# Other orders for the matmuls of the block products and of two mixer stages

## The chip, the core and the metric

The kernel runs on one core of one Trainium2 chip. The metric is the device time of one execution in microseconds, the median of several runs. TensorE (PE) does the matmuls, VectorE (DVE), ScalarE (ACT) and GpSimd (POOL) the elementwise work, SyncE (SP) issues DMAs. All engines run their own instruction streams and meet at semaphores.

## The reference

One layer of a streaming encoder, in fp32, for a prompt of 512 frames and 64 frames of a running stream, 1024 features:

```python
def encoder_layer(x, hist_a, hist_b, ...):
    x = x + 0.5 * swiglu_ffn(rms_norm(x, ffn1_norm), ffn1_w_gate_up, ffn1_w_down)
    h = rms_norm(x, mix_norm)
    p = h @ w_in
    a_b, a_c, a_v, b_u, gate_a, gate_b = jnp.split(p, cuts, axis=-1)
    a_conv, new_a = causal_depthwise_conv(a_c * a_v, hist_a, conv_a_w)
    y_a = (a_b * a_conv) @ w_a_out
    glu = b_u[..., :D_B] * jax.nn.sigmoid(b_u[..., D_B:])
    b_conv, new_b = causal_depthwise_conv(glu, hist_b, conv_b_w)
    b_act = jax.nn.silu(layer_norm(b_conv + conv_b_bias, conv_b_ln_g, conv_b_ln_b))
    y_b = b_act @ w_b_out
    merged = jax.nn.sigmoid(gate_a) * y_a + jax.nn.sigmoid(gate_b) * y_b
    x = x + merged @ w_out
    x = x + 0.5 * swiglu_ffn(rms_norm(x, ffn2_norm), ffn2_w_gate_up, ffn2_w_down)
```

A final `rms_norm` follows. `D_FF` is 2816; `w_in` has seven blocks of 1024 columns. The histories of both convolutions are outputs too.

## The kernel before

Features lie on the 128 rows, the T = 576 frames on the columns, in two halves of H = 288 columns (`HALVES`). An input `X[j]` is one of KT = 8 tiles of 128 features. To keep fp32 accuracy with the fast fp32r matmul, each operand is split into a high and a low part, and a product is the sum of three: high weights times high input, high weights times low input, low weights times high input. In the code these are `parts` 0, 1 and 2, or `m` 0, 1 and 2.

An ordinary product (`product`, `mm`) makes 128 output features for both halves. It takes the 8 feature tiles of its input one after the other, and for each runs six matmuls, part n on half s, in the order `SIX`: (0,0), (1,0), (0,1), (1,1), (2,0), (2,1). The first half adds into one PSUM bank, the second into the next bank of the same tile. Each such product has 48 matmuls of 288 columns in the FFN's first tiles and in the mixer, and 30 or 36 in the down projections.

The mixer's stages are: `("p", 4, j)` and `("p", 3, j)` for branch B; `("p", 1, j)`, `("p", 2, j)` and `("p", 0, j)` for branch A, 24 products; `("p", 5, j)` with `("ya", j)`; `("p", 6, j)`, 8 products; `("yb", j)`; `("o", j)`. Between some of them a sum over features is made with four matmuls against a tile of ones (`Sum.total`).

The gate and up products of the FFNs work in pairs (`pair`): for output tile i, both parts together are made from seven block products over half the feature tiles (KU = 4), a scheme of the Strassen kind. Each block product has a weight unit of its own, streams one half of the columns into one bank, and has twelve matmuls: four tiles k times three parts m. `Forms.operands` says which half each of the seven streams: first, second, first, first, first, second, second, in the order in which they run. The FFN's 22 output tiles form four groups (`GROUPS`: 5, 5, 6 and 6); the first 3 tiles of the first FFN and the first tile of the second are ordinary products (`PLAIN`). After each group the down projection of that group runs.

Weights come through `Stream`: SyncE loads a raw unit of 256 KB, ScalarE casts the high part, and the low part is made either by VectorE or, for units marked "dma", by ScalarE negating the high part and GpSimd issuing a DMA that adds the raw weights to it. `ws.get(n)` prepares six units ahead of the one asked for. All instructions stay in program order on their engine (`Ordered`); `dve.time` and `pe.time` are a planner's counts that decide when work put off (`work`, `behind`) is placed. They depend on the number and width of the matmuls, not on their order.

Where the profile names L80, that is the helper through which all instructions are recorded; buffers are told apart by name: `mm` are PSUM tiles, `act` are inputs (and in the mixer also weights), `u` and `g` are weights.

Of the kernel before, what the change touches and what calls it, by code (L numbers as in the profile page):

```python
# [17 lines left out]
FT = DFF // P  # L18
SEQ = 512
DSEQ = 64  # L20
KU = KT // 2
# [23 lines left out]
HALVES = ((0, H), (H, T))  # L45
# [8 lines left out]


SIX = ((0, 0), (1, 0), (0, 1), (1, 1), (2, 0), (2, 1))

RAWS = 6

# [44 lines left out]
def tile_encoder_step(  # L104
# [284 lines left out]
    plan_ffn("f2", ffn2_gu, ffn2_dn)  # L389


    def mm(ps, w, kk, xs, first, last, spans=HALVES):


        (whi, wlo), (xh, xl) = w, xs
        parts = ((whi, xh), (whi, xl), (wlo, xh))
        for n, s in SIX:
            if s < len(spans):
                (a, b), (i, e) = parts[n], spans[s]
                pe.matmul(  # L400
                    ps[:, s, : e - i], a[:, kk, :], b[:, i:e],
                    start=first and n == 0, stop=last and n == 2,
                )

    def chunks(name):
# [25 lines left out]
    def product(name, xs, then=None, order=None, got=None):  # L431

        if name in early:
            return early.pop(name)[:, :, :H]
        ps = psum2()
        if order or got:
            got = got or chunks(name)
            for n, k in enumerate(order or range(len(xs))):
                mm(ps, *got[k], xs[k], n == 0, n == len(xs) - 1)
        else:  # L440
            k = 0
            for n in plan[name]:
                w = ws.get(n)
                for kk in range(ws.units[n][1]):
                    mm(ps, w, kk, xs[k], k == 0, k == len(xs) - 1)
                    k += 1
        take()
        if then is None:
            dve.time = max(dve.time, pe.time)
            return ps[:, :, :H]  # L450
        fill()
        behind.append((pe.time, lambda: then(ps[:, :, :H])))
# [205 lines left out]
    first = {name: psum2() for name in FIRST}  # L658
# [31 lines left out]
    def ffn(f, xg, sums, finish, forms, R=None, todo=()):  # L690
# [41 lines left out]
                for step, p in todo.pop(0):  # L732
                    step(p)

        def pair(i, hs, last):
            qu, uu, t, cu = (ttile() for _ in range(4))
            q1, u2, u3, u4 = half(qu, 0), half(qu, 1), half(uu, 0), half(uu, 1)
            q = []

            def q7():  # L740
                dve.tensor_tensor(u3, q[3], u2, op=ALU.add)
                dve.tensor_tensor(half(cu, 1), u3, q[2], op=ALU.subtract)

            def gate():
                dve.tensor_tensor(half(t, 1), q[5], u4, op=ALU.add)
                dve.tensor_tensor(t, t, R, op=ALU.mult)
                sca.activation(t, t, AF.Silu)

            steps = (
                lambda: sca.copy(q1, q[0]),  # L750
                lambda: dve.tensor_tensor(u2, q[1], q1, op=ALU.subtract),
                lambda: dve.tensor_tensor(u4, q[2], u2, op=ALU.subtract),
                q7,
                lambda: dve.tensor_tensor(half(t, 0), q[4], q1, op=ALU.add),
                gate,
            )
            for n, xs in enumerate(bs):
                w = ws.get(plan[f, "s", i][n])
                q.append(bank()[:, :H])
                for k in range(KU):  # L760
                    (whi, wlo), (xh, xl) = w, xs[k]
                    for m, (l, r) in enumerate(((whi, xh), (whi, xl), (wlo, xh))):
                        pe.matmul(
                            q[n], l[:, k, :], r, start=k == m == 0, stop=k == KU - 1 and m == 2
                        )
                if n > 0:
                    steps[n - 1]()
                if rest:
                    rest.pop(0)()

            hs.append(None)
            at = len(hs) - 1

            def up():
                if last:
                    dve.tensor_tensor(t, t, R, op=ALU.mult)
                dve.tensor_tensor(half(cu, 0), q[6], u3, op=ALU.add)

            def hidden():
                dve.tensor_tensor(cu, cu, t, op=ALU.mult)  # L780
                hs[at] = high(cu)

            def parts():
                hs[at] = hs[at], low(cu, hs[at])

            rest.extend((up, hidden, parts))

        for g, grp in enumerate(GROUPS):
            hs = []
            for i in grp:  # L790
                if i < PLAIN[f]:
                    plain(i, hs)
                    continue
                if i == PLAIN[f]:
                    bs = forms.operands(xg)
                pair(i, hs, grp[-1] == FT - 1)
            while rest:
                rest.pop(0)()
            spare.clear()
            if grp[-1] < FT - 1:  # L800
                for j, ps in enumerate(both([(f, "d", g, j) for j in range(2)], hs)):
                    update(j, ps, R)
                for j in range(2, KT):
                    update(j, product((f, "d", g, j), hs), R)
            else:
                finish(g, hs)
# [390 lines left out]
```

## Time and profile before

| | us |
|---|---|
| median of 3 runs | 1302.38 (1302.33 to 1303.26) |
| profiled execution | 1303.07 |
| its span | 1301.3 |
| TensorE busy | 1286.3 |
| VectorE busy | 892.0 |
| ScalarE busy | 778.5 |
| GpSimd busy | 400.5 |

The span runs from the first to the last instruction; the rest of an execution's time lies around it. The granted clock of TensorE was 0.998 of full speed. A row of the list of stretches gives start and end in us from the span's start, the length, TensorE's busy time and the number of matmuls that touch the stretch, the granted clock, the share of the DMA engines and GB/s. A row of time gives start, length, engine, line, operation, tiles and the number of instructions merged in it. A matmul's own length (some 294 ns) contains its passage through the pipeline, so speed is read from start to start or from a stretch's length over its matmuls.

### The profile page before, as it was taken

Reading aid. Unit: us, or ns where it says so; the run is one execution under the profiler, and the core shown is the slowest. Engines: PE = TensorE matmul, PEld = TensorE weight load, DVE = VectorE, ACT = ScalarE, POOL = GpSimd, SP = SyncE. Lnnn points to the kernel's source line nnn. Section 1 sums busy time; section 2 is a strip of 40 time slices with the busy share of each in tenths; the row PEclk is TensorE's granted clock in tenths of the full one; section 3 lists DMA queues with packets and bytes.
Section 4 is the critical chain, followed back from the end, with each engine's and each line's share of the span. In section 5 each row is a group of like instructions: output and inputs, shape, how many; then the busy total and the mean of one; then the engine's idle time right before and its main releaser. Section 6 shows DMA issues by size and latency. Waiting matters only on the chain.

```text
span 1301.3 us, 25714 instructions
## 1 busy us (share of the span) xinstructions
PE 1286.3 (99%) x9746; PEld 1282.5 (99%) x9746; DVE 892.0 (69%) x1460; ACT 778.5 (60%) x1374; POOL 400.5 (31%) x502
## 2 busy tenths in 40 slices
PE   9999999999999999999999999999999999999997
PEld 8999999999999999999999999999999999999996
DVE  6758758748945899888895260336967848847955
ACT  8755655645677655555554684457665655654664
POOL 4242332332242544322221322222142141241233
PEclk9999999999999999999999999999999999999999
DMA  9797787886798797877775978776687796796784
GB/s 245 141 189 160 148 185 157 165 192 147 152 195 182 167 216 173 175 166 170 172 168 125 199 158 178 154 166 142 138 169 165 162 192 149 163 206 136 161 178 107
DMA packets 290108, 218.40 MB, mean 168 GB/s; under 512 B 15680, under 2 KB 251200, under 8 KB 289984
## 3 DMA queue, kind: packets, MB, share of 16 engines
q0 software_dynamic: 60768, 100.30, 46.4%
q1 hardware_dynamic: 227488, 115.62, 31.4%
q8 instruction: 77, 1.26, 0.4%
q10 hardware_dynamic: 1728, 0.84, 0.2%
q14 instruction: 47, 0.39, 0.1%
HBM read 113.81 MB, written 2.62 MB: 89 GB/s over the span
## 4 chain that ended last, share of the span: by engine, by line
PE 90%; issue 4%; DMA 2%; ACT 1%; POOL 1%; DVE 1%; DVEq 0%; POOLq 0%; ACTq 0%; SPq 0%
PE mm L80 90%; DMA g<-raw 1%; DMA raw<-in_ffn_w_gate_up_dram 1%; POOL act L80 1%; DVE tmp L80 0%; ACT u L80 0%; DMA gains<-in_params_dram 0%; POOL g L80 0%; ACT tmp L80 0%; ACT g L80 0%; DVE acc L80 0%; ACT act L80 0%; DVE x L80 0%; DVE g L80 0%; POOL tmp L80 0%
## 5 line engine op out<-in xcount | busy, mean ns | idle before, releaser
L80 PE MATMUL mm<-act,u 128*128 128x288 f32 x4686 | 660.9, 294 | 0.7 <-DVE u L80 0.5
L80 PEld LDWEIGHTS mm<-act,u 128*128 128x128 f32 x4686 | 630.9, 188 | 1.2 <-DVE u L80 0.7
L80 PE MATMUL mm<-act,g 128*128 128x288 f32 x2766 | 398.6, 294 | 2.1 <-DMA g<-raw 2.0
L80 PEld LDWEIGHTS mm<-act,g 128*128 128x128 f32 x2766 | 376.5, 188 | 2.9 <-DMA g<-raw 2.8
L80 POOL DMA_DIRECT2D u<-raw x204 | 176.3, 864 | 550.4 <-ACT u L80 492.2
L80 PE MATMUL mm<-act,act 128*128 128x288 f32 (+2 forms) x2244 | 307.6, 293 | 1.4 <-DVE act L80 1.4
L80 PEld LDWEIGHTS mm<-act,act 128*128 128x128 f32 x2244 | 297.8, 188 | 2.4 <-DVE act L80 2.1
L80 POOL DMA_DIRECT2D g<-raw x124 | 108.6, 876 | 247.2 <-ACT g L80 188.2
L80 ACT CAST u<-raw 128x512 fp32r<-128x512 f32 (+2 forms) x204 | 117.1, 574 | 108.6 <-PE mm L80 76.5
L80 DVE SCALAR_TENSOR_TENSOR w<-g,prm,w 128x606 f32<-128x606 f32 x232 | 179.3, 844 | 1.4 <-ACT w L80 1.4
L80 DVE TENSOR_TENSOR tmp<-mm,tmp 128x288 f32<-128x288 f32 (+1 forms) x244 | 109.7, 458 | 72.9 <-PE mm L80 53.5
L80 ACT ACTIVATE u<-u 128x512 fp32r<-128x512 f32 (+2 forms) x204 | 121.1, 594 | 6.5
L80 POOL DMA_DIRECT2D act<-raw x90 | 78.9, 876 | 50.6 <-ACT act L80 49.5
L80 DVE SCALAR_TENSOR_TENSOR tmp<-mm,r 128x576 f32<-128x576 f32 x48 | 36.3, 757 | 78.0 <-PE mm L80 77.8
L80 ACT CAST g<-raw 128x512 fp32r<-128x512 f32 (+2 forms) x124 | 67.7, 546 | 35.3 <-DMA raw<-in_ffn_w_down_dram 14.7
L80 ACT CAST act<-tmp 128x576 fp32r<-128x576 f32 x84 | 56.2, 674 | 52.4 <-DVE tmp L80 51.6
L80 ACT CAST g<-w 128x512 fp32r<-128x512 f32 x80 | 49.6, 619 | 63.0 <-DVE w L80 56.6
L80 ACT CAST u<-w 128x512 fp32r<-128x512 f32 x80 | 49.5, 619 | 61.9 <-DVE w L80 55.7
L80 DVE TENSOR_TENSOR act<-tmp,act 128x576 fp32r<-128x576 f32 x80 | 59.3, 754 | 21.3 <-ACT act L80 19.8
L80 ACT ACTIVATE g<-g 128x512 fp32r<-128x512 f32 (+2 forms) x124 | 70.4, 568 | 3.9
L80 ACT CAST act<-raw 128x512 fp32r<-128x512 f32 (+2 forms) x99 | 57.6, 583 | 16.1 <-PE mm L80 11.0
L80 DVE TENSOR_TENSOR w<-raw,raw 128x512 f32<-128x512 f32 x80 | 54.8, 685 | 11.0 <-DMA raw<-in_ffn_w_gate_up_dram 11.0
(88 smaller groups left out, 814.1 us busy)
## 6 DMA issues: line engine op xcount, KB each, us to landing
raw<-in_ffn_w_gate_up_dram SPq DMA_DIRECT2D x173, 256.0 KB, 3.4
u<-raw POOLq DMA_DIRECT2D x145, 256.0 KB, 4.0
raw<-in_w_in_dram SPq DMA_DIRECT2D x112, 256.0 KB, 3.4
act<-raw POOLq DMA_DIRECT2D x80, 256.0 KB, 4.8
raw<-in_ffn_w_down_dram SPq DMA_DIRECT2D x96, 192.0 KB, 3.5
g<-raw POOLq DMA_DIRECT2D x65, 256.0 KB, 3.8
g<-raw POOLq DMA_DIRECT2D x43, 192.0 KB, 4.5
u<-raw POOLq DMA_DIRECT2D x43, 192.0 KB, 4.5
```

Source lines behind the costliest of these rows:

```text
L80: return self.tc.keep_in_program_order(fn(*args, **kwargs))
```

## The change

The order of matmuls becomes a parameter. `mm` takes `six`; the three branch-A stages `("p", 1)`, `("p", 2)`, `("p", 0)` get `BACK`, the stage `("p", 6)` gets `PAIRED`, all others keep `SIX`. `pair` takes `twelve`, one order for each group of each FFN. The first group of the first FFN gets `BY_TILE`, which is the order of before. The flags that open and close an accumulation follow the order.

```diff
+BACK = ((0, 0), (1, 0), (1, 1), (0, 1), (2, 1), (2, 0))
+PAIRED = ((0, 0), (1, 0), (0, 1), (1, 1), (2, 1), (2, 0))
+
+BY_TILE = tuple((k, m) for k in range(KU) for m in range(3))
+SAME_INPUT = tuple((k, m) for k in range(KU) for m in (0, 2, 1))
+TO_AND_FRO = tuple((k, m) for k in range(KU) for m in ((1, 0, 2), (2, 0, 1))[k % 2])
+LOW_LAST = tuple((k, m) for ms in ((0, 1), (2,)) for k in range(KU) for m in ms)
+BY_PART = tuple((k, m) for m in range(3) for k in range(KU))
+LOW_FIRST = tuple((k, m) for k in range(KU) for m in (2, 0, 1))
+TWELVE = {
+    "f1": (BY_TILE, SAME_INPUT, TO_AND_FRO, LOW_LAST),
+    "f2": (BY_PART, LOW_FIRST, SAME_INPUT, TO_AND_FRO),
+}
...
-    def mm(ps, w, kk, xs, first, last, spans=HALVES):
+    def mm(ps, w, kk, xs, first, last, spans=HALVES, six=SIX):
         (whi, wlo), (xh, xl) = w, xs
         parts = ((whi, xh), (whi, xl), (wlo, xh))
-        for n, s in SIX:
+        opens = {s: n for n, s in reversed(six)}
+        closes = {s: n for n, s in six}
+        for n, s in six:
             if s < len(spans):
                 (a, b), (i, e) = parts[n], spans[s]
                 pe.matmul(
                     ps[:, s, : e - i], a[:, kk, :], b[:, i:e],
-                    start=first and n == 0, stop=last and n == 2,
+                    start=first and n == opens[s], stop=last and n == closes[s],
                 )
...
-                    mm(ps, w, kk, xs[k], k == 0, k == len(xs) - 1)
+                    six = {("p", 1): BACK, ("p", 2): BACK, ("p", 0): BACK, ("p", 6): PAIRED}
+                    mm(ps, w, kk, xs[k], k == 0, k == len(xs) - 1, six=six.get(name[:2], SIX))
...
-                for k in range(KU):
-                    (whi, wlo), (xh, xl) = w, xs[k]
-                    for m, (l, r) in enumerate(((whi, xh), (whi, xl), (wlo, xh))):
-                        pe.matmul(
-                            q[n], l[:, k, :], r, start=k == m == 0, stop=k == KU - 1 and m == 2
-                        )
+                whi, wlo = w
+                for at, (k, m) in enumerate(twelve):
+                    xh, xl = xs[k]
+                    l, r = ((whi, xh), (whi, xl), (wlo, xh))[m]
+                    pe.matmul(q[n], l[:, k, :], r, start=at == 0, stop=at == len(twelve) - 1)
...
-                pair(i, hs, grp[-1] == FT - 1)
+                pair(i, hs, grp[-1] == FT - 1, TWELVE[f][g])
```

The instructions of VectorE, ScalarE, GpSimd and SyncE stand in the same order as before. Two places on TensorE show what moves. The first is the seventh block product of the second pair of the second FFN (group order `BY_PART`): the out tile, the streamed input, the weights; `g_11646` is the high and `g_11647` the low part of the weights, made by DMA. Before:

```order
L80 MATMUL mm_11760<-act_10932,g_11646 128x288
L80 MATMUL mm_11760<-act_11092,g_11646 128x288
L80 MATMUL mm_11760<-act_10932,g_11647 128x288
L80 MATMUL mm_11760<-act_11088,g_11646 128x288
L80 MATMUL mm_11760<-act_11254,g_11646 128x288
L80 MATMUL mm_11760<-act_11088,g_11647 128x288
```

And now, to the first with the low part:

```order
L94 MATMUL mm_11760<-act_10932,g_11646 128x288
L94 MATMUL mm_11760<-act_11088,g_11646 128x288
L94 MATMUL mm_11760<-act_11250,g_11646 128x288
L94 MATMUL mm_11760<-act_11339,g_11646 128x288
L94 MATMUL mm_11760<-act_11092,g_11646 128x288
L94 MATMUL mm_11760<-act_11254,g_11646 128x288
L94 MATMUL mm_11760<-act_11343,g_11646 128x288
L94 MATMUL mm_11760<-act_11347,g_11646 128x288
L94 MATMUL mm_11760<-act_10932,g_11647 128x288
```

The low part of the weights was read by the third matmul and is now read by the ninth.

The second place is the first product of branch A, `("p", 1, 0)`, order `BACK`, the first of its eight feature tiles; `u_6356` and `u_6357` are the high and low part of the weights, `act_5411` and `act_5419` those of the first input tile, and a row with x2 is the same pair of tiles on one half and then on the other. Before:

```order
L80 MATMUL mm_6576<-act_5411,u_6356 128x288
L80 MATMUL mm_6576<-act_5419,u_6356 128x288
L80 MATMUL mm_6576<-act_5411,u_6356 128x288
L80 MATMUL mm_6576<-act_5419,u_6356 128x288
L80 MATMUL mm_6576<-act_5411,u_6357 128x288 x2
```

And now:

```order
L94 MATMUL mm_6576<-act_5411,u_6356 128x288
L94 MATMUL mm_6576<-act_5419,u_6356 128x288 x2
L94 MATMUL mm_6576<-act_5411,u_6356 128x288
L94 MATMUL mm_6576<-act_5411,u_6357 128x288 x2
L94 MATMUL mm_6576<-act_5414,u_6356 128x288
```

The low part of the input is now streamed on both halves in a row, and the high part on the second half with both parts of the weights in a row. The halves, which the rows don't show, run first, first, second, second, first, second before, and first, first, second, second, second, first now. `PAIRED` has the same sequence of halves; its rows read like those of `SIX`, with the two matmuls of the x2 row exchanged.

2 lines of the change are left out of this document (1 added, 1 removed).

## The prediction

> **What bounds the kernel now.** I read the page first: the shares, then who waits for whom, then the speed of the bounding engine stage by stage.
>
> ```profile
> span 1301.3 us, 25714 instructions
> PE 1286.3 (99%) x9746; PEld 1282.5 (99%) x9746; DVE 892.0 (69%) x1460; ACT 778.5 (60%) x1374; POOL 400.5 (31%) x502
> ...
> PEclk9999999999999999999999999999999999999999
> ```
>
> TensorE is busy in 99% of the span; VectorE, next, in 69%. There are 9746 weight loads for 9746 matmuls: each matmul loads its weights, also where they are those of the matmul before. The list of waits of TensorE, whole span:
>
> ```profile
> PE mm L80 <- DMA g<-raw: 2.0, 2, 1.5
> PE mm L80 <- DVE act L80: 1.7, 3, 0.8
> PE mm L80 <- POOL eps L80: 1.0, 1, 1.0
> PE mm L80 <- DVE acc L80: 0.5, 1, 0.5
> PE mm L80 <- DVE u L80: 0.5, 1, 0.5
> ```
>
> All of it is 5.7 us. So an order of matmuls can act in two ways: on a wait, or on the spacing of matmuls that follow without one. For the spacing I took stretches that begin and end with a stage, whose matmuls the program counts (the counts in the rows have two or three more, which overlap the edges; the first number after the stretch is its length):
>
> ```profile
> 105.77:161.37 55.60, 55.60 (x422) 1.00 0.70 149
> 192.98:259.70 66.72, 66.72 (x506) 1.00 0.73 156
> 364.34:402.26 37.92, 37.92 (x290) 1.00 0.96 197
> 409.11:502.71 93.60, 93.60 (x722) 1.00 0.86 181
> 502.71:652.47 149.76, 149.76 (x1155) 1.00 0.79 171
> 652.47:696.15 43.68, 43.68 (x338) 1.00 0.77 162
> 696.69:721.97 25.28, 25.28 (x195) 1.00 0.53 110
> 753.70:803.62 49.92, 49.92 (x387) 1.00 0.81 169
> 803.62:903.46 99.84, 99.84 (x771) 1.00 0.74 158
> 1267.31:1279.71 12.40, 12.40 (x93) 1.00 0.66 119
> 1281.19:1287.85 6.66, 6.66 (x56) 1.00 0.15 49
> ```
>
> - Block products, two groups of the first FFN: 55.60/420 and 66.72/504, both 132.4 ns a matmul.
> - The down projection behind them, order SIX: 37.92/288 = 131.7 ns.
> - Mixer, order SIX: 93.60/720, 149.76/1152, 43.68/336, 49.92/384 and 99.84/768, all 130.0 ns.
> - Four mixer products from 696.69, same order SIX, same kinds of operands: 25.28/192 = 131.7 ns. They stand between two sums over features, of four matmuls each. So one order has two rhythms, 130.0 and 131.7, and a disturbance of four matmuls moves it from one to the other.
> - The two last rows are the last products, 304 and 272 columns wide: 12.40/90 = 137.8 and 6.66/54 = 123.3 ns.
>
> What makes the block products dearer? One pair of block products, TensorE's row of time:
>
> ```profile
> 1004.17 1.74 PE L80 MATMUL mm<-act,g 128*128 128x288 f32 x12
> 1005.74 1.76 PE L80 MATMUL mm<-act,u 128*128 128x288 f32 x12
> 1007.34 1.74 PE L80 MATMUL mm<-act,g 128*128 128x288 f32 x12
> 1008.92 1.74 PE L80 MATMUL mm<-act,u 128*128 128x288 f32 x12
> 1010.50 1.74 PE L80 MATMUL mm<-act,g 128*128 128x288 f32 x12
> 1012.09 1.76 PE L80 MATMUL mm<-act,u 128*128 128x288 f32 x12
> 1013.69 1.76 PE L80 MATMUL mm<-act,g 128*128 128x288 f32 x12
> 1015.29 0.29 PE L80 MATMUL mm<-act,u 128*128 128x288 f32 x1
> ```
>
> From start to start the seven take 1.57, 1.60, 1.58, 1.58, 1.59, 1.60, 1.60 us. In the code the second, sixth and seventh stream the second half (288 columns further in the same tiles), the others the first half. First half: 1.58/12 = 131.7 ns; second half: 1.60/12 = 133.3 ns. The order of weights and inputs is the same in all seven, so it does not make this difference; the place of the streamed half does. And the first-half products, in which 4 of 12 matmuls repeat the weights, cost the same 131.7 ns as SIX in the down projection, where 4 of 6 repeat them. I read from this: what sets the spacing is the sequence of halves and a rhythm into which it falls, not which operand is repeated.
>
> **The change part by part.** On VectorE, ScalarE, GpSimd and SyncE the built order is the same row for row, DMA issues included; no wait is added. TensorE has the same matmuls, 4728 of them in stretches whose order may change.
>
> *Block products, 3192 matmuls in seven groups (the first group of the first FFN keeps its order).* All twelve of a product stream one half into one bank, in any order. So the sequence of halves stays as it is. I take 0. Bounds from the nearest rows: 130.0 at the cheap end, 3192 x (130.0 - 132.4) = -7.6 us; all at 133.3, +3.0 us. Could a matmul now wait? The order that opens with the low part of the weights needs it 2 matmuls sooner, 0.26 us; the one with the low part second, 0.13 us. The one wait in a changed group says how near the low parts run (first the chain of waits, start and length in us, then TensorE's row of time):
>
> ```profile
> 928.93 4.44 issue
> 933.37 0.01 POOLq L80
> 933.38 4.34 DMA g<-raw
> 937.72 0.04 issue
> 937.77 2.26 PE mm L80 x15
> ```
>
> ```profile
> 935.72 1.63 PE L80 MATMUL mm<-act,u 128*128 128x288 f32 x11
> 937.19 2.17 PE L80 MATMUL mm<-act,g 128*128 128x288 f32 x12
> 939.21 1.08 PE L80 MATMUL mm<-act,u 128*128 128x288 f32 x7
> ```
>
> That is the second pair of the second FFN, seventh product: 2.02 us (937.19 to 939.21) instead of 1.60, so 0.42 us of waiting, for a low part whose DMA was issued at 933.38 and took 4.34 us. This group now takes the low part of the weights last, from the ninth matmul instead of the third: it is needed at 937.19 + 8 x 0.133 = 938.26 us, 0.5 us after it has landed. The wait goes: -0.42 us. Next in line is the following pair, which runs 0.42 us sooner and whose low parts are also needed 0.8 us later. In the groups where the low part is needed sooner, the list of waits has nothing, and weights are prepared six units ahead, six products of about 1.6 us; a DMA of a low part takes about 4 us:
>
> ```profile
> u<-raw POOLq DMA_DIRECT2D x145, 256.0 KB, 4.0
> g<-raw POOLq DMA_DIRECT2D x65, 256.0 KB, 3.8
> ```
>
> 9.5 us less some 4 us, less the queueing ahead of the issue, covers 0.26 us; if that cover were gone each of 35 products would pay at most 0.26 us, 9 us in all.
>
> *The two mixer stages, 1152 + 384 = 1536 matmuls.* Here the sequence of halves does change. SIX runs first, first, second, second, first, second. Both new orders run first, first, second, second, second, first, and then begin again with first: runs of three, two changes of half (and of bank) in six matmuls instead of four. The trace has no such sequence. Bounds: at the cheap end no row of 288 columns is below 130.0; since nothing excludes a better rhythm I allow one step of the size seen, 1.67 ns: 1536 x -1.67 = -2.6 us. At the dear end all at 133.3: 1536 x 3.33 = +5.1 us. Between: SIX's own second rhythm, 131.7 (+1.67 x 1536 = +2.6 us), and the mean of the long runs, (131.7 + 133.3)/2 = 132.5 (+3.8 us). Fewer changes bring the sequence away from the fast rhythm and towards the long runs; three is nearer to SIX's runs of two than to twelve. I take 131.7: +2.6 us.
>
> *What follows the two stages* is unchanged in order, but may fall into the other rhythm, as at 696.69. Of the stage behind the first, 576 matmuls now run at 130.0 and 192 at 131.7; a swap costs (576 - 192) x 1.67 = +0.6 us. Behind the second 816 run at 130.0: +1.4 us. I take 0 for both and keep +2.0 for the range; below, the 192 at 131.7 can gain 0.3.
>
> Sum: 0 - 0.42 + 2.6 = +2.2 us. The profiled execution took 1303.07 us, 1.8 more than its span, and the median of the runs is 1302.38. Span after: 1303.5; median 1304.5 us, +0.17%.
>
> **The rivals.**
>
> 1. *The runs of three cost what long runs cost* (slower). Place: the two mixer stages; price 132.5 - 130.0 = 2.5 ns x 1536 = +3.8, less 0.42: 1305.8 us, and 1307.8 if both stages behind also swap rhythm. It decides for slower from a spacing of 132.0 ns on ((2.6 + 0.42)/1536 = 2.0 ns above 130.0). For it: the long-run rows; against it: SIX was never above 131.7.
> 2. *The order does not matter in the mixer either*; only the wait goes: 1302.0 us. For it: four of each six matmuls keep their place; against it: the half did matter in the block products. The Trainium skill (TensorE: Matmul & The Clock Gate, "Back-to-back issue gap") gives the isolated spacing by the column count alone, which would leave every order equal; this trace has 130.0, 131.7 and 133.3 ns at 288 columns and does not agree.
> 3. *Repeated operands matter*, in either direction. Of 3192 block matmuls the change takes 420 repeats of weights away (105 products, four each) and adds 784 repeats of the input. At the largest difference among the 288-column rows, 3.33 ns: +1.4 us for the first, -2.6 us for the second; if whole groups with repeated input (2352 matmuls) went to 130.0, 2352 x 2.4 = -5.6 us, 1296.4 us with the mixer as now. Against it: equal spacings at 4 repeats in 12 and 4 in 6. The same page of the Trainium skill ("Step-by-step: what each phase is for") says that weights stay put over many matmuls, so that one load serves several; the counts, one load a matmul, show that this program doesn't get that.
>
> **How the numbers follow.** A measurement of this kernel tells about 0.2%, 2.6 us, from no change. Forecast (mixer at 131.3 to 132.0): 0.45, own range 1303.9 to 1305.9. Rival 1: 0.27. Rival 2, or a mixer below 131.3: 0.20. Rival 3: 0.08, in halves. Slower by over 2.6 us: rival 1, a fourth of the forecast (where a stage behind swaps), a part of rival 3: 0.42. Faster: 0.06. Same: 0.52. The range runs from 1301.0 (rival 2 with a step to spare) to 1307.8 (rival 1 with both swaps).
>
> **What would show it.** In the profile after: the stretches of the block products unchanged at 132.4 ns in all groups, whatever the order; their first-half products 1.58 us and second-half 1.60. No wait at the second pair of the second FFN, and none new. The stage of 1152 matmuls at about 152.3 us instead of 149.76, that of 384 at 50.6 instead of 49.92. The prediction is wrong if a block group departs from 132.4 ns, if the two mixer stages stay at 130.0, or if they pass 132.0.

## The result: 0.8% slower, nearly all of it in the mixer

| | before | after |
|---|---|---|
| median | 1303.26 us (1302.33 to 1304.18, 5 runs) | 1313.36 us (1312.92 to 1313.77, 5 runs) |
| span of the profiled execution | 1301.3 us | 1311.4 us |

The ratio is 1.0077, with a 95% interval of 1.0066 to 1.0088. The forecast was 1304.5 us with a range up to 1307.8, so the time lies outside it.

The page of the changed kernel, span and shares:

```profile
span 1311.4 us, 25728 instructions
PE 1296.5 (99%) x9746; PEld 1292.7 (99%) x9746; DVE 892.0 (68%) x1460; ACT 777.7 (59%) x1374; POOL 400.8 (31%) x502
```

TensorE has the same 9746 matmuls and is busy 10.2 us longer (before: 1286.3). The busy time of the other engines is as it was, to 0.8 us. The waits of TensorE, as before us in total, times, longest:

```profile
PE mm L94 <- DMA g<-raw: 2.7, 3, 1.5
PE mm L94 <- DVE act L94: 1.7, 3, 0.8
PE mm L94 <- POOL eps L94: 1.0, 1, 1.0
PE mm L94 <- DVE acc L94: 0.3, 1, 0.3
```

They add up to 5.7 us, as before. So all of the loss is spacing of matmuls that wait for nothing. The stretches by stage in the changed kernel (start and end, length, busy time and matmuls that touch it, granted clock, DMA share, GB/s):

```profile
106.04:161.64 55.60, 55.60 (x423) 1.00 0.73 150
193.24:259.96 66.72, 66.72 (x507) 1.00 0.73 156
409.37:502.97 93.60, 93.60 (x723) 1.00 0.86 181
502.97:656.55 153.58, 153.58 (x1154) 1.00 0.78 167
656.55:701.72 45.17, 45.17 (x339) 1.00 0.76 157
702.25:727.53 25.28, 25.28 (x194) 1.00 0.51 106
759.26:810.45 51.19, 51.19 (x387) 1.00 0.80 165
810.45:913.69 103.24, 103.24 (x770) 1.00 0.72 154
927.00:971.48 44.48, 44.48 (x339) 1.00 0.72 151
```

The first group of the second FFN, the last of these rows, stood so in the kernel before:

```profile
916.55:961.45 44.90, 44.75 (x339) 1.00 0.73 152
```

Set beside the stretches that the prediction shows, in the order of the program:

| stage | matmuls | before, us | after, us | difference | after, ns a matmul |
|---|---|---|---|---|---|
| block products, groups two and three of the first FFN | 924 | 122.32 | 122.32 | 0 | 132.4 |
| branch B, order SIX | 720 | 93.60 | 93.60 | 0 | 130.0 |
| branch A, order `BACK` | 1152 | 149.76 | 153.58 | +3.82 | 133.3 |
| behind it, to the first sum, SIX | 336 | 43.68 | 45.17 | +1.49 | 134.4 |
| between the two sums, SIX | 192 | 25.28 | 25.28 | 0 | 131.7 |
| stage `("p", 6)`, order `PAIRED` | 384 | 49.92 | 51.19 | +1.27 | 133.3 |
| `("yb")` and `("o")`, SIX | 768 | 99.84 | 103.24 | +3.40 | 134.4 |
| from there to the first group of the second FFN | | 13.09 | 13.31 | +0.22 | |
| that group, `BY_PART` | 336 | 44.90 | 44.48 | -0.42 | 132.4 |

Together +9.78 of the 10.1 us of span; of the rest, 0.27 had come before the first of these stretches (106.04 against 105.77), where the order is the same. Half of the loss, 5.09 us, lies in the two stages whose order changed. The other half, 5.11 us, lies in work behind them whose order did not change. It ran at 134.4 ns, which no row of the kernel before has. (The 13.31 us hold one product of 48 matmuls at 134.4 ns, up to the next sum over features.)

The block products kept their speed by the half, and the wait at the seventh product of the second pair of the second FFN is gone. The row of time there (start, length):

```profile
947.64 1.76 PE L94 MATMUL mm<-act,g 128*128 128x288 f32 x12
949.24 1.74 PE L94 MATMUL mm<-act,u 128*128 128x288 f32 x12
```

The seventh, from 947.64, takes 1.60 us to the next start, where it had taken 2.02.

### The profile page after: what moved, and what is told of

The parts are those of the page before. It is cut to its first block, busy times and chain, and to the rows that moved or that the text cites. A ratio compares the mean times of both kernels' runs of the same rounds, so it can differ in the third digit from the quotient of the medians.

```text
span 1311.4 us, 25728 instructions
## 1 busy us (share of the span) xinstructions
PE 1296.5 (99%) x9746; PEld 1292.7 (99%) x9746; DVE 892.0 (68%) x1460; ACT 777.7 (59%) x1374; POOL 400.8 (31%) x502
## 4 chain that ended last, share of the span: by engine, by line
PE 94%; ACT 2%; issue 1%; DMA 1%; DVE 1%; POOL 0%; DVEq 0%; SPq 0%; POOLq 0%; ACTq 0%
PE mm L94 94%; DMA g<-raw 1%; DMA raw<-in_ffn_w_gate_up_dram 0%; ACT act L94 0%; ACT tmp L94 0%; DVE tmp L94 0%; POOL act L94 0%; DMA gains<-in_params_dram 0%; ACT u L94 0%; ACT w L94 0%; ACT L94 0%; ACT g L94 0%; DVE acc L94 0%; DVE g L94 0%; DVE w L94 0%
## 5 line engine op out<-in xcount | busy, mean ns | idle before, releaser
L94 PE MATMUL mm<-act,act 128*128 128x288 f32 (+2 forms) x2244 | 313.1, 295 | 1.5 <-DVE act L94 1.5
L94 PEld LDWEIGHTS mm<-act,act 128*128 128x128 f32 x2244 | 302.8, 188 | 2.7 <-DVE act L94 2.4
L94 DVE TENSOR_TENSOR w<-raw,raw 128x512 f32<-128x512 f32 x80 | 54.8, 685 | 10.2 <-DMA raw<-in_ffn_w_gate_up_dram 10.2
```

The lines of the kernel that those rows point to most:

```text
L94: return self.tc.keep_in_program_order(fn(*args, **kwargs))
```

## Experiments

Unless something else is said, each kernel computes all of the reference. Spans are those of the profiled execution and stand against 1301.3 us of the kernel before. A time that comes from one run is to be read against 1302.3 to 1304.8 us, the spread of single runs of the kernel before. A rhythm is the spacing into which a repeating order of matmuls has settled.

### One part of the change at a time

The block orders alone (all mixer stages in SIX):

```diff
-six = {("p", 1): BACK, ("p", 2): BACK, ("p", 0): BACK, ("p", 6): PAIRED}
+six = {}
```

> The seven block groups take their new orders, the mixer keeps the order of before. Theory H (the sequence of streamed halves, and the rhythm it falls into, sets the spacing): every block group keeps its length, 55.60 us for 420 matmuls and 66.72 for 504; only the wait at the second pair of the second FFN goes, -0.4 us, which a measurement can't tell from no change. Theory O (repeated operands set it): the groups whose orders take weight repeats away, or add input repeats, would differ from 132.4 ns a matmul, by up to 3.3 ns on those repeats; the changed kernel's own trace already speaks against it.

1302.68 us (1302.33 to 1303.55) against 1302.93, ratio 0.9998 (0.9988 to 1.0007); span 1301.0. Every block group and every mixer stage has the length of before, and the first group of the second FFN is 0.41 us shorter. 3192 matmuls in five new orders, and none of them changed its spacing.

Branch A alone, and the fourth stage alone (blocks as before):

```diff
-six = {("p", 1): BACK, ("p", 2): BACK, ("p", 0): BACK, ("p", 6): PAIRED}
+six = {("p", 1): BACK, ("p", 2): BACK, ("p", 0): BACK}      # branch A alone
+six = {("p", 6): PAIRED}                                    # fourth stage alone
```

> Only the 24 products of branch A take the order BACK; blocks and the gate stage p6 as before. Theory H: that stage 153.6 us instead of 149.76 (133.3 ns), and the 336 unchanged matmuls behind it 134.4 instead of 130.0 ns, +1.5 us, up to the next sum over features; behind that all as before, the p6, yb and o stages at 49.92 us each. In all +5.3 us, 0.4%. Rival D (the slow rhythm behind is made by something else in the program, not by the stage ahead of it): the yb and o stages would be slow here too.

> Only the 8 products of p6 take the order PAIRED. Theory H: p6 51.2 us instead of 49.92, yb and o behind it 51.6 each instead of 49.92, about +4.9 us in all; branch A and the stage behind it as before (149.76 and 101.2 us). PAIRED repeats no input and as many weights as SIX, so theory O expects p6 at 49.92 us and no change. Rival D: yb and o at 49.92.

Branch A alone: 1308.53 us, ratio 1.004 (1.0025 to 1.0055). Its stretches (branch A; behind it to the first sum; `("p", 6)`; `("yb")` and `("o")`):

```profile
502.98:656.57 153.59, 153.59 (x1155) 1.00 0.78 167
656.57:701.73 45.16, 45.16 (x338) 1.00 0.75 157
...
759.27:809.19 49.92, 49.92 (x386) 1.00 0.82 169
809.19:909.03 99.84, 99.84 (x770) 1.00 0.74 159
```

The fourth stage alone, one run: 1308.37 us. Its `("p", 6)`, and `("yb")` with `("o")`:

```profile
753.65:804.84 51.19, 51.19 (x387) 1.00 0.78 165
804.84:908.08 103.24, 103.24 (x770) 1.00 0.72 154
```

Each part brings its own loss and the one behind it: +3.83 and +1.48 from branch A, +1.27 and +3.40 (and 0.21 in the product after it) from the fourth stage. What branch A leaves behind ends at the sums over features: the stages from 759.27 on are at 130.0 ns. What `("p", 6)` leaves behind runs through two stages, since no sum lies between them. The two losses add up.

### Is it the sequence of halves, or the operands?

Three other orders in the same four stages, blocks as before (f is the first half, s the second):

```diff
+MIXED = ((2, 0), (1, 0), (2, 1), (1, 1), (0, 0), (0, 1))      # same_halves: f f s s f s
+ALT = ((0, 0), (0, 1), (1, 0), (1, 1), (2, 0), (2, 1))        # alternating: f s f s f s
+REVERSED = ((0, 0), (1, 0), (0, 1), (2, 0), (1, 1), (2, 1))   # reversed:    f f s f s s
```

`MIXED` has the halves of SIX and other parts: the weights change four times in six matmuls, where SIX changes them twice.

> Blocks as before; branch A and p6 take an order that runs over the halves as SIX does (first, first, second, second, first, second) but with other parts in each place: low weights with high input first, then high weights with low input, on both halves, then high with high. The weights are repeated at 2 of 6 matmuls instead of 4. Theory H: 130.0 ns as before, 149.76 and 49.92 us, nothing behind moves, no change in the time. Theory O: fewer repeats of weights cost something, 130.0 to 133.3 ns, up to +5 us.

> Blocks as before; branch A and p6 run the halves strictly in turn, first, second, first, second, first, second, so six changes in six matmuls instead of four; weights are repeated at 5 of 6. Theory H, in the form that each change of half gives a chance to save (no saving in runs of three, 3 steps of 6.67 ns in six for SIX): at or below 130.0 ns, down to 128.3; the two stages 149.76 us and 49.92 us or less. Theory O (more repeats of weights save): also below 130.0. Theory R (only the rhythm entered counts, not the number of changes): any of 130.0, 131.7, 133.3.

> The addresses of before; branch A and p6 run the halves first, first, second, first, second, second: the order of halves of SIX read backwards, with the same four changes and the same runs of two and one. Theory H1 (number of changes and lengths of runs set the price): 130.0 or SIX's other rhythm, 131.7. Theory H2 (it depends on the very sequence): any of 130.0 to 133.3; strictly alternating halves, six changes, cost 133.3, so more changes are not cheaper.

The order with the halves of SIX (1303.14 us; branch A, and the two stages behind `("p", 6)`, which itself took 49.92 us):

```profile
502.48:652.24 149.76, 149.76 (x1155) 1.00 0.80 170
...
803.38:903.22 99.84, 99.84 (x770) 1.00 0.74 158
```

To the hundredth the stretches of before. The alternating order (1310.89 us; branch A, behind it to the first sum, between the two sums, `("p", 6)`, the two behind). Its weights come in the sequence of SIX, four repeats in six matmuls and not the five that its expectation counts, so what it changes is the sequence of streamed inputs:

```profile
503.06:656.64 153.58, 153.58 (x1154) 1.00 0.78 167
656.64:700.88 44.24, 44.24 (x338) 1.00 0.76 160
701.42:726.70 25.28, 25.28 (x195) 1.00 0.53 109
...
758.43:809.61 51.18, 51.18 (x386) 1.00 0.80 165
809.61:910.73 101.12, 101.12 (x770) 1.00 0.73 157
```

The reversed order (1307.25 us) in branch A:

```profile
502.50:654.20 151.70, 151.70 (x1155) 1.00 0.78 167
```

Four sequences, three prices in these stages: SIX 130.0; reversed 131.7; alternating and the runs of three 133.3. The operand that repeats does not matter. The number of changes of half does not order them either: SIX and the reversed order both have four, the alternating one six, the runs of three two. Each new sequence had its price in both stages (50.58/384 = 131.7 ns for the reversed one in `("p", 6)`), but nearly always entered from work at 130.0 ns. SIX itself is seen at three spacings, so a price belongs to a sequence together with the way into it; only for `PAIRED` is another way in seen, from 131.7 ns, again at 133.3 (51.19 us, in the kernel with the idle matmuls below).

And what lies behind, always SIX, depends on where it comes from: 134.4 ns behind the runs of three, 131.7 (44.24/336, 101.12/768) behind the alternating and, to 0.01 us, the reversed order.

### Why a half has a price: the place, not the bank

In the block products, first half and second half differ by 1.8 ns a matmul (131.6 and 133.4, as means over 17 pairs; the prediction's 131.7 and 133.3 come from rounded rows). They differ in the place that is streamed and, from pair to pair, in the bank that is written. One kernel runs the third and the fourth block product, both on the first half, matmul by matmul in turn, into two banks:

```diff
 for n, xs in enumerate(bs):                # was: seven block products, one after the other
+    ns = (2, 3) if n == 2 else (n,)        # the third and the fourth together
...
+            for a, w in zip(ns, wn):
+                pe.matmul(q[a], l[:, k, :], r, ...)
```

> The mixer as before. In every pair the third and fourth block product, which both stream the first half, run interleaved, so that the bank of the output changes at every matmul while the half stays. In SIX half and bank change together; this separates them. Theory H (half of the input): the 24 matmuls still take 3.16 us (131.7 ns each), block groups 55.60 and 66.72 us. Theory B (the change of bank makes the saving): 130.0 ns or less for these 24, 40 ns a pair, 1.6 us in all.

1319.89 us, 17 us slower, though not through the spacing there. The first group that consists of such pairs alone:

```profile
108.77:164.37 55.60, 55.60 (x422) 1.00 0.71 148
```

55.60 us, as before: a change of bank at every matmul costs nothing. The loss has two other places. The second unit of weights is asked for twelve matmuls sooner, and waits for weights appear, above all in the down projections; behind the longest, 2.7 us, the granted clock was 0.63 from 1268.00 to 1272.50 us, with matmuls up to 240 ns apart. Outside the mixer the kernel loses 11.1 us, most of it so:

```profile
PE mm L80 <- DMA g<-raw: 4.2, 2, 2.7
PE mm L80 <- DMA u<-raw: 3.4, 3, 1.5
```

And all 1872 matmuls of both branches, all in SIX as before, ran at 131.7 ns:

```profile
413.09:507.89 94.80, 94.80 (x722) 1.00 0.86 181
507.89:659.57 151.68, 151.68 (x1154) 1.00 0.78 167
```

That is +3.1 us in the two branches and +2.6 in the stages behind, in a mixer in which nothing was edited: the rest of the 17 us. The experiments on the rhythm, below, take this up.

Next, the place. The input tiles (`act`) were moved by 32, 64, 96 or 128 bytes against the weights by a small tile that nothing reads, ahead of their pool, and a second one behind it that makes up 256 bytes, so that the weights in `u` and `g` stay where they were modulo 256. In the mixer the weights of every second unit (24 matmuls) lie in `act` tiles and move along:

```diff
+gap1 = ctx.enter_context(tc.tile_pool(name="gap1", bufs=1))   # 32, 64, 96 or 128 bytes
 act = ctx.enter_context(tc.tile_pool(name="act", bufs=44))
+gap2 = ctx.enter_context(tc.tile_pool(name="gap2", bufs=1))   # 224, 192, 160 or 128 bytes
```

and, for comparison, inputs and weights together by 32 bytes (a tile `pad` among the constants, ahead of all their pools).

> The kernel of before with all input tiles moved by 128 bytes on their rows (an unused tile ahead of their pool and one behind, so that the other weights stay where they were). The halves are 1152 bytes apart, 4.5 times 256, so the first half now stands where the second stood, modulo 256 bytes. Theory A (it is the address modulo 256 that makes the second half dearer): block products change places, first half 1.60 us and second 1.58, so a pair takes 4 x 1.60 + 3 x 1.58 = 11.14 us instead of 11.12 and a group of 420 matmuls 55.70 instead of 55.60. Theory N (the half has its price from its place in the tile, not from its address): 55.60 and 1.58 for the first half.

> The kernel of before with every tile moved by 32 bytes, so that the first halves of inputs and all weights begin at a multiple of 256 bytes and the second halves at a multiple of 128; before they began 32 bytes ahead of that. If reads go in lines of 64 bytes, 288 columns touch 18 lines instead of 19: theory A expects a step of 6.67 ns less for a matmul at most, 123.3 to 130 ns everywhere, up to -60 us. Theory N: 1303 us.

> The kernel of before with the input tiles 32 bytes further; weights in u and g stay. Moving everything by 32 bytes changed nothing and moving the inputs alone by 128 made the halves change places, so theory W says: what counts is where the input begins relative to the weights, modulo 256 bytes (first half 0, second 128 before: 131.7 and 133.3 ns; here 32 and 160). It expects block products that differ from both, between 130.0 and 133.3 ns. Theory L (lines of 64 bytes count too, 128 was a multiple of them): a change of the price in both halves, also outside 130.0 to 133.3. Null: 1.58 and 1.60 us as before.

> The same with 64 bytes: first half 64, second 192 beyond the weights, modulo 256. Theory W: block products differ from 1.58 and 1.60 us; if reads of weights and input meet in one of four places 64 bytes apart, both halves are away from the weights by one place and either spacing can fall to 130.0 ns (1.56 us a product) or rise to 133.3 (1.60).

> The same with 96 bytes: first half 96, second 224 beyond the weights, modulo 256. Theory W: if only the place in steps of 64 counts, as with 64 bytes; if 32 counts, a price of its own.

Inputs and weights by 32 bytes (1303.23 us; first changed block group, branch A):

```profile
105.93:161.53 55.60, 55.60 (x422) 1.00 0.68 149
...
502.86:652.62 149.76, 149.76 (x1154) 1.00 0.78 170
```

Nothing moved. Inputs alone by 32 bytes (1316.27 us; block group, branch A):

```profile
106.80:162.80 56.00, 56.00 (x422) 1.00 0.70 148
...
507.73:659.57 151.84, 151.84 (x1154) 1.00 0.77 167
```

Block products 133.3 ns, the mixer 131.8. Inputs alone by 128 bytes (1310.32 us), second to fourth product of a pair:

```profile
108.20 1.74 PE L80 MATMUL mm<-act,u 128*128 128x288 f32 x12
109.78 1.76 PE L80 MATMUL mm<-act,g 128*128 128x288 f32 x12
111.38 1.76 PE L80 MATMUL mm<-act,u 128*128 128x288 f32 x12
```

Here the product from 108.20 streams the second half and takes 1.58 us to the next start; the one from 109.78 streams the first half and takes 1.60. Means over the 17 pairs of groups two to four of the first FFN and over the stages, in ns a matmul, with one run each:

| inputs moved by | first half | second half | down projection | mixer, SIX | time, us |
|---|---|---|---|---|---|
| 0 | 131.6 | 133.4 | 131.7 | 130.0 | 1303 |
| 32 bytes | 133.4 | 133.2 | 133.3 | 131.8 | 1316.27 |
| 64 bytes | 132.1 | 133.3 | 133.3 | 131.3 | 1311.94 |
| 96 bytes | 131.8 | 133.5 | 133.3 | 132.8 | 1316.73 |
| 128 bytes | 133.4 | 131.6 | 131.7 | 131.7 | 1310.32 |

With 128 bytes the two halves exchange their prices. The second half begins 288 x 4 = 1152 bytes behind the first, which is 128 modulo 256: moving the inputs by 128 puts the second half where the first was.

The mixer column mixes two kinds of matmuls, and that makes a test within one run. Branch A with the inputs moved by 32 bytes, weights in `u`, which stayed, and in `act`, which moved along:

```profile
520.38 3.36 PE L80 MATMUL mm<-act,u 128*128 128x288 f32 x24
523.58 3.29 PE L80 MATMUL mm<-act,act 128*128 128x288 f32 x24
526.71 3.36 PE L80 MATMUL mm<-act,u 128*128 128x288 f32 x24
```

The same inputs take 3.20 us for 24 matmuls with the weights against which they moved (133.2 ns over the stage), and 3.13 with those that moved along (130.4). In the kernel before both kinds take 3.12. With 64 bytes the two are at 132.3 and 130.3 ns. With 96 and 128 bytes the second kind leaves 130.0 as well (132.2 and 132.0); whether it takes that over from the unit before it, these runs don't separate.

So a half's price comes from the place of the streamed input relative to the weights, and a sequence of halves is a sequence of two such places. The Trainium skill (SBUF — State Buffer, "A bandwidth-pool intuition that's wrong (but worth ruling out)") gives weight loads a read port of their own beside that of the streamed operand, by which the two would not disturb each other. The rows don't fit that conclusion: moving one against the other costs up to 13.7 us, moving both costs nothing. What meets where inside the chip, no run shows.

### The third rhythm is a state that lasts

Four matmuls against a tile of ones, as in a sum, two on the first half and two on the second, were put into the changed kernel ahead of the stage behind branch A and ahead of `("yb")`; nobody reads their result.

```diff
+def idle_four():
+    t = psum2()
+    for s in range(2):
+        for n in range(2):
+            pe.matmul(t[:, s, :H], ones_r, half(xg[0][0], s), start=n == 0, stop=n == 1)
+idle_four()          # ahead of the stage ("p", 5), and ahead of ("yb")
```

> The changed kernel with four more matmuls, in the halves first, first, second, second and with a result that nobody uses, ahead of the stage behind branch A and ahead of the one behind the fourth stage of the change (ya's companion stage is the first, yb the second). Theory (a rhythm is kept since the entry into a stage and a short disturbance ends it): the 336 matmuls at 134.4 ns behind branch A and the 768 at 134.4 ns of yb and o go to 131.7 or to 130.0; yb and o together from 103.2 to 101.1 or 99.8 us, the stage behind branch A from 45.2 to about 44.2 us; the two disturbances cost some 0.53 us each; the span 1311.4 - 0.9 - 2.1 + 1.1 = 1309.5 us or somewhat less. Rival (134.4 ns belongs to what lies behind a run of three, for example to the place of the weights or to the PSUM banks, and comes back): yb and o stay at 103.2 us and the span rises by 1.1 to 1312.5 us.

One run: 1310.83 us, span 1309.1 against 1311.4 of the changed kernel. Behind branch A, between the sums, and `("yb")` with `("o")`:

```profile
656.79:701.04 44.25, 44.25 (x338) 1.00 0.76 159
701.57:726.54 24.97, 24.97 (x195) 1.00 0.49 100
...
810.38:911.51 101.13, 101.13 (x771) 1.00 0.73 157
```

Both stages leave 134.4 for 131.7 ns, 0.92 and 2.11 us less, for two times 0.52 us of idle matmuls. So 134.4 ns does not belong to the place or the stage; it is a rhythm that was entered behind the runs of three and kept. Runs of three are not the only way into it: in the kernel with the third and fourth block product together, six products of one down projection, all in SIX, ran at it (29.04/216 = 134.4):

```profile
1168.16:1197.20 29.04, 29.04 (x218) 1.00 0.83 178
```

Four matmuls at the entry avoid it, and in the changed kernel the four of the first sum ended it (45.17 us ahead of the sum, 25.28 us at 131.7 ns behind it). The row between the sums shows more: it was 25.28 us at 131.7 ns and is now 24.97 at 130.0. The stretch ahead of the first sum is now at 131.7, where it had been at 130.0 or 134.4. In this kernel each sum exchanged 131.7 and 130.0.

That is not a rule. In the 15 kernels whose inputs did not move against the weights, four sums each stand between stages in SIX. 130.0 ns became 131.7 at all 21 sums that it met, 134.4 became 131.7 at all 4, and 131.7 became 130.0 at 31; but at 4 sums, two each behind the alternating and the reversed order, 131.7 stayed 131.7 (44.24 and 25.28 us above). So one spacing can be two states, and the spacing alone does not tell what comes next.

### Can the rhythm be chosen?

The down projections run at 131.7 ns in the kernel before. If they could be brought to 130.0, each would gain 0.4 to 0.5 us. First attempt: one single set of six matmuls in another order, in six of them, as a nudge.

```diff
+NUDGE = {("f1", 0): ((0, 0), (0, 1), (1, 0), (1, 1), (2, 0), (2, 1)), ...}   # six entries
...
+nudge = name[1] == "d" and name[3] == 2 and k == 0
+mm(ps, w, kk, xs[k], k == 0, k == len(xs) - 1, six=NUDGE.get((name[0], name[2]), SIX) if nudge else SIX)
```

> The kernel before, with one single set of six matmuls in another order of halves in each of six down projections (first tile of the third product): first FFN groups one to three: first, second, first, second, first, second; second, second, first, second, second, first (by its own sequence); and others in the rest. All else as before. Theory (131.7 and 130.0 ns are two states of one order, and one disturbance can choose): some of the six down projections leave 131.7 ns for 130.0 from their third product on, -0.4 to -0.5 us each; span 1301.3 - 0.4 x their number, so 1298.7 to 1301. A nudge that sends one to 133.3 or 134.4 would cost as much. Rival (the rhythm of a down projection is set by its tiles, not by its past): all six stay at 131.7 ns and the span at 1301.3 us.

(In the edit the second of these sequences is second, second, first, first, second, first.)

1303.40 us, ratio 1.0004 (0.9994 to 1.0013). None of the six is at 130.0 afterwards. But the first stood there before its nudge, since in this run a wait in its first products happened to end in that rhythm (the thirty matmuls ahead of the nudged product, and the 150 behind it):

```profile
78.51:82.41 3.90, 3.90 (x33) 1.00 1.01 211
86.36:106.11 19.75, 19.75 (x152) 1.00 0.91 199
```

130.0 ahead of it (3.90/30), 131.7 behind (19.75/150). So the end of a wait chooses a rhythm too, and not the same one in each run: the profiled execution of the kernel before has 131.7 there. A set of alternating halves took it from the cheap rhythm to the dear one; five others left 131.7 ns behind them as it was.

Second attempt: run the block products themselves in the sequence of SIX, the first together with the second and the fifth with the sixth.

```diff
+TOGETHER = (0, 4)
...
+first, second = ws.get(at), ws.ready.pop(at + 1)
+for k in range(KU):
+    for m, a in SIX:
+        (whi, wlo), (xh, xl) = (first, second)[a], bs[n + a][k]
```

> The kernel before, with the first and second and the fifth and sixth block product of each pair run together, matmul by matmul, in the sequence of halves first, first, second, second, first, second; the pair's third, fourth and seventh product stay alone. Theory (the sequence of halves sets the spacing, whatever the banks and the weights): the 48 matmuls run together go from 132.5 ns to 130.0 or 131.7; 40 pairs x 48 x 2.5 = -4.8 us or x 0.8 = -1.6 us, less what the earlier need of the second unit's weights costs in waits (up to 6 us, if waits for a DMA appear as they did where the third and fourth were run together). Rival (block products run at 132.4 ns in any arrangement, for their tiles): no change or slower by the waits alone.

1308.11 us, ratio 1.0038 (1.0024 to 1.0051). The first pair of the first such group (first and second product together; fifth and sixth together), then the first two together of the next pair:

```profile
106.09:109.21 3.12, 3.12 (x27) 1.00 0.26 39
...
112.36:115.49 3.13, 3.13 (x27) 1.00 0.90 227
...
117.09:120.25 3.16, 3.16 (x26) 1.00 0.30 60
```

The same block products that ran at 132.4 ns run at 130.0 (3.12/24) in the sequence of SIX. So their tiles do not bind them to 132.4, and another sequence of halves changes the spacing there as well. But behind the seventh product, which stands alone on the second half, the next pair is at 131.7 (3.16/24), and later products run together are between 131.7 and 132.5: the whole group of five pairs gains 0.16 us, where 130.0 ns throughout would have given 5 x 48 x 2.4 = 0.6. And the mixer paid for it. In the last down projection ahead of it two matmuls start 0.38 us apart, a delay of 0.25 us, behind which the rhythm was 130.0, and the sum behind it turned the mixer to 131.7 (rest of that down projection, branch B):

```profile
369.48:402.24 32.76, 32.76 (x255) 1.00 0.97 197
409.02:503.82 94.80, 94.80 (x723) 1.00 0.85 180
```

The mixer then loses 5.7 us, as it did with the third and fourth block product together: there too this down projection ran at 130.0 behind a wait, of 0.9 us.

Third attempt: shift the sequence itself. One product of a down projection begins with a few matmuls more, and takes what is then left of each half at its end; no matmul more or less. Five forms in five places.

```diff
+TURN = {("f1", 1): ("llhh", "lh"), ("f1", 2): ("lh", "llhh"), ("f2", 0): ("llh", "hlh"),
+        ("f2", 1): ("ll", "hhlh"), ("f2", 2): ("l", "lhhlh")}      # l first half, h second
...
+halves = turn[0] + "llhhlh" * (len(xs) - 1) + turn[1]
```

> The kernel before, with the third product of five down projections begun at another place in its sequence of halves: before the usual first, first, second, second, first, second stand (A) first, first, second, second; (B) first, second; (C) first, first, second; (D) first, first; (E) first; and what is then too much of each half is taken at the product's end. First FFN groups two and three have A and B, second FFN groups one to three have C, D and E. No matmul more or less. Theory (131.7 and 130.0 ns are two states of one order and four matmuls first, first, second, second exchange them, as the sums over features do): A leaves 131.7 ns for 130.0, -0.3 us, if what is taken at the end doesn't bring it back; of the others perhaps one. Rival (the state is bound to where the down projection's tiles lie): all five stay at 131.7 and the span at 1301.3 us.

One run, 1303.08 us. The five products behind the shifted one in the down projection of the first FFN's second group (form A), and the same in the second FFN's second group (form D):

```profile
173.27:192.77 19.50, 19.50 (x152) 1.00 0.86 194
...
1060.67:1080.17 19.50, 19.50 (x153) 1.00 0.94 206
```

19.50/150 = 130.0 ns instead of 131.7. Behind A and D the rhythm of 130.0 holds. B reached 130.0 in its product and fell back at its end; C and E came out at 131.7. Then D at all five places, with the block orders of the change and SIX in the mixer:

> The block orders of the change, all mixer stages in the order SIX, and in five down projections the third product's matmuls begun with two more of the first half (the form D that left 131.7 ns for 130.0 in the first FFN's or second FFN's one place where it stood). Theory (the five down projections enter that product in the same phase, so D acts in all of them): five times about -0.3 us (180 to 216 matmuls behind it at 130.0 instead of 131.7, less the 0.01 us that D itself costs), with the wait at the second pair of the second FFN gone at most -0.4 more: span 1299.4 us, ratio 0.9986. Rival (D worked by the phase of that one place): only second FFN group two gains, span 1300.6 to 1301.0 us, ratio 0.9995 to 0.9998.

1302.07 us (1301.36 to 1302.84, 11 runs) against 1303.12 (15 runs), ratio 0.9991 (0.9982 to 1.0000). D worked in the three down projections of five feature tiles, -0.24 us each, and in none of the two with six, which came out at 131.7 (23.70/180). There the shifted product is six matmuls longer; why that matters is not shown. With the wait gone (0.41 us) that makes 1.1 us. In the profiled execution, 1301.1 us of span, most of this is hidden, since it reached the first of these stretches 0.8 us later than the kernel before (173.99 against 173.23). This is the lowest median seen, and it is not told from the kernel before with certainty.

## Why the prediction was wrong

*Block products, "I take 0"*: right, to 0.01 us a group, and for the reason given: all twelve stream one half, so the sequence of halves stays. The block orders alone show it, and the mixer order with other parts and the same halves shows it from the other side (rival 3 falls).

*The wait in the second FFN, "The wait goes: -0.42 us"*: measured -0.42. The new order was free of it in all four kernels that had it (44.48 us in each). With the old order the group took between 44.48 and 45.31 us from run to run, so the gain is 0 to 0.8, and 0.42 belongs to the one execution; that it came out so exactly is luck.

*The two mixer stages, "I take 131.7: +2.6 us"*: the mechanism was right and the size wrong. The sequence of halves changed the spacing, but runs of three cost 133.3 ns, the dear end of the bounds: +5.09 us. By the prediction's own sign ("or if they pass 132.0") this too counts against it. What led astray was the reasoning from the number of changes of half, "three is nearer to SIX's runs of two than to twelve". The alternating order has the most changes and costs 133.3 too. Nothing in the trace of before priced a new sequence. Rival 1 had the right place and direction, with 132.5 ns.

*What follows the two stages, "I take 0 for both and keep +2.0 for the range"*: this step failed, and it is the larger miss. It saw that a stage inherits a rhythm, but took the two rhythms on view for all there are. Behind a run of three a third one held, 134.4 ns, for 336 and for 768 matmuls: +5.11 us with the product after them. With this term at 0 and the mixer term as measured the prediction's own sum is 1302.38 + 5.09 - 0.42 = 1307.05 us, inside the range. (Taken off the measured median it is 1313.36 - 5.11 = 1308.25, just outside, since the kernel before was at 1303.26 in that comparison.)

*The range, up to 1307.8*: it joined the +2.0 with rival 1's 132.5 ns and not with the dear end, 133.3, that the prediction had set itself. With both, 1302.38 - 0.42 + 5.1 + 2.0 = 1309.1 us, it would still have missed.

*Rival 2*, that the order does not matter in the mixer, falls by +3.83 us of branch A alone. The Trainium skill's isolated spacing by the column count (TensorE: Matmul & The Clock Gate, "Back-to-back issue gap"), which is given there for a single matmul and not for a stream, would leave all orders equal: at 288 columns and a granted clock of 1.00 the rows now show 130.0, 131.7, 133.3 and 134.4 ns, so it does not agree.

## What to carry to other kernels

Where TensorE is busy for 99% of the span, the order of matmuls counted here through the sequence of places that it streams and not through the operands that it repeats. Such an order had states, and an edit is paid for in the unedited work behind it, until something ends the state. So read the spacing stage by stage, also where nothing was edited, and give a stage that inherits its rhythm a wide bound upward. A good state reached by chance (this mixer at 130.0 ns) can be lost behind a delay of 0.25 us in the stage ahead of it; the mixer then took 5.7 us more, over twenty times as much.

## What was not expected of the hardware

- One order of six matmuls of 288 columns ran at 130.0, 131.7 or 134.4 ns a matmul, at a granted clock of 1.00, and kept its rhythm over up to 2208 matmuls (720, 1152 and 336 in the kernel before, all at 130.0).
- Four matmuls of a sum moved it from one rhythm to another at 56 of 60 sums, and behind a wait or a shorter delay it was seen at 130.0 and at 131.7. A sum took 130.0 and 134.4 to 131.7, and 131.7 to 130.0 except behind the alternating and the reversed order.
- The place of the streamed input against the weights, in steps of 32 bytes, changes the time by up to 13.7 us, or 1%; the common place of both, moved by 32 bytes, does not. Within one run the same inputs took 133.2 ns with weights that stood still and 130.4 with weights that moved along.
- One and the same shift of the sequence took three down projections with five feature tiles to 130.0 ns and left two with six at 131.7. Why a given sequence has its price, and which rhythm it falls into from a given past, stays open: the runs give prices and not a rule.
